# A three-block model in split float32: two of the three products of each up projection and gate joined in one 512-column product

## The chip, the cores and the metric

The kernel runs on one core of a Trainium2 chip. The metric is the device time of one execution in microseconds. The program is one launch that loads all its weights from device memory.

## The reference

Three blocks of width 1024 run over one sequence of 256 tokens, each a mixer followed by a feed-forward. The first mixer holds two attentions over 8 heads, one that keeps 64 keys for each query (picked by an index score) and one over low-rank keys and values; sigmoid gates weigh the two branches:

```python
        y_a = jnp.einsum('bsc,cd->bsd', o_a, w_branch_a[l])
        y_b = jnp.einsum('bsc,cd->bsd', o_b, w_branch_b[l])
        merged = jax.nn.sigmoid(g_a) * y_a + jax.nn.sigmoid(g_b) * y_b
        h = h + jnp.einsum('bsd,de->bse', merged, w_out[l])

        hn = rmsnorm(h, norm_ffn_g[l])
        u = jnp.einsum('bsd,df->bsf', hn, w_up[l])
        u = causal_depthwise_conv(u, conv_w[l], conv_b[l])
        gate, val = jnp.split(u, 2, axis=-1)
        h = h + jnp.einsum('bsf,fd->bsd', jax.nn.silu(gate) * val, w_down[l])
```

The second mixer is a gated linear recurrence, the third an attention with a bias by distance. Their feed-forwards are silu(gate) * val without the convolution. Each feed-forward has 2816 columns of gate and 2816 of val.

## The kernel before, in words

Everything is kept transposed: 128 features on the partitions, 256 tokens along the free axis. A matrix of activations `X` is eight row blocks of [128, 256].

*Split products.* Weights and activations are float32. `Weights` loads a piece of 1024 columns, and cuts it into a high part `H` (a ScalarE copy to float32r) and a low part `L` (a VectorE subtraction); these are the "weight splits" below, 128x1024 rows written to tiles named `r`. Activations are cut in the same way by `hl`. A product then is three TensorE instructions (`mm3`): weight high with activation high, weight high with activation low, weight low with activation high, all summed in PSUM. Each has a weight load of its own.

```python
        m(ps, lhsT=aH, rhs=bH, start=start, stop=False, skip_group_check=True)
        m(ps, lhsT=aH, rhs=bL, start=False, stop=False, skip_group_check=True)
        m(ps, lhsT=aL, rhs=bH, start=False, stop=stop, skip_group_check=True)
```

*Projections.* `proj_t` makes 256 output features: eight row blocks times two column blocks times three products of 256 columns, 48 in all, into one PSUM bank (two halves of 256). There are 8 banks.

*The feed-forward.* `ffn` goes over 11 blocks. `up(j)` projects 256 columns of gate and then 256 of val, scales by 1/rms (`rb2`), applies the convolution in the first block's feed-forward (`conv`), the silu, and multiplies; the result is cut in two parts, `acts[j]`. `down(j)` multiplies 256 rows of the down weights with it into accumulators that stay open over the whole stage: four banks of two halves in the first two feed-forwards, five banks in the last (`final`), which is computed token by token, with 512- and 256-column products. The code says up(j) and then down(j - 1).

*The order of instructions.* The program is recorded first, and `Trace.schedule` puts it in order: a list scheduler that goes by a rough price for each instruction, takes what comes earliest in the recorded order among what is ready on an engine, and gives out buffers (15 `f4`, 23 `r4`, 10 `f2`, 8 `ps`, ...) as they come free. So any change in the recorded work moves other instructions as well. All of them carry one line number in the profile, 428, where they are emitted.

*A store in the first mixer.* `late_setup` makes a table of biases by distance for the third mixer: an 8x384 row in an `f2` buffer, spread by a GpSimd DMA to 1.5 MB in device memory (`dram`). It is recorded after the first mixer, and scheduled among its attentions.

## Time and profile before

| | before |
|---|---|
| time, median of 3 runs | 1055.04 us (1054.74 to 1059.61) |
| span of the profiled execution | 1055.1 us |
| TensorE busy (products) | 1015.7 us, 96% |
| VectorE busy | 720.5 us, 68% |
| ScalarE busy | 533.0 us, 51% |
| TensorE's mean granted clock | 0.987 |

The profiled execution is seen by its span, from its first to its last instruction. A product's own duration is longer than its distance to the next, since products overlap in the engine; a pace has to be read from a count of them in a known time.

The stages in the span: first mixer up to about 227 us, the feed-forward with convolution to about 420, the recurrence to about 576, the second feed-forward to about 757, the third mixer to about 863, the last feed-forward to the end.

### The profile page before, as it was taken

To read this page: it belongs to the slowest core of one execution; us is meant where nothing else is said; L and a number is where in the kernel's file an instruction comes from. 1 tells how busy PE (TensorE), PEld (TensorE's weight loads), DVE (VectorE), ACT (ScalarE), POOL (GpSimd) and SP (SyncE) were. 2 spreads that over 40 slices of the span, in tenths; PEclk is the share of its full clock that TensorE was granted. 3 is DMA by queue.
4 is the path that set the end of the run, shared out by engine and by line. 5 is a ranking of instruction groups with operands and counts; after the bars stand their busy time and mean duration, and the time that the engine had idled before them with its cause. 6 is when DMAs were issued, how large, how long until landed. Compare 5 with 4: busy or idle time off the path is not lost.

```text
span 1055.1 us, 20892 instructions
## 1 busy us (share of the span) xinstructions
PE 1015.7 (96%) x8710; PEld 973.7 (92%) x8710; DVE 720.5 (68%) x1278; ACT 533.0 (51%) x804; POOL 44.7 (4%) x40
## 2 busy tenths in 40 slices
PE   7998499999999999999999999999999999999997
PEld 5876399999999999999999999999989999999996
DVE  7996256768867779887878655555856676556564
ACT  7867244546555557444455444444544655444322
POOL 2000000020000002000002000000200010000000
PEclk9999599999999999999999999999999999999999
DMA  9347355745555565355555565656555555565501
GB/s 325 94 125 164 98 161 160 250 150 163 189 189 183 177 200 160 101 162 167 168 176 153 178 200 162 199 172 197 167 164 174 177 162 178 171 207 171 162 1 40
DMA packets 130688, 174.02 MB, mean 165 GB/s; under 512 B 6163, under 2 KB 113043, under 8 KB 130593
## 3 DMA queue, kind: packets, MB, share of 16 engines
q1 hardware_dynamic: 129312, 169.31, 50.9%
q0 software_dynamic: 1280, 3.37, 1.7%
q8 instruction: 68, 1.11, 0.4%
q14 instruction: 28, 0.22, 0.1%
HBM read 170.04 MB, written 2.62 MB: 164 GB/s over the span
## 4 chain that ended last, share of the span: by engine, by line
PE 88%; DVE 5%; DMA 4%; ACT 1%; POOL 1%; issue 1%; POOLq 0%; DVEq 0%; ACTq 0%
PE ps L428 88%; DMA dram<-f 3%; DVE r L428 3%; DVE f L428 2%; POOL f L428 1%; ACT f L428 1%; DVE fs L428 1%; DVE h L428 1%; DMA f<-in_conv_w_dram 0%; ACT r L428 0%; DVEq L428 0%; POOLq L428 0%; DVE lb L428 0%; ACTq L428 0%; POOLq L1412 0%
## 5 line engine op out<-in xcount | busy, mean ns | idle before, releaser
L428 PE MATMUL ps<-r,r 128*128 128x256 f32 (+3 forms) x7182 | 938.7, 291 | 3.1 <-DVE r L428 2.3
L428 PEld LDWEIGHTS ps<-r,r 128*128 128x128 f32 x7182 | 898.5, 192 | 25.6 <-DVE r L428 4.6
L428 ACT ACTIVATE r<-f 128x1024 fp32r<-128x1024 f32 (+4 forms) x369 | 352.4, 989 | 211.5 <-DVE f L428 100.9
L428 DVE TENSOR_TENSOR r<-f,r 128x1024 fp32r<-128x1024 f32 (+3 forms) x365 | 411.8, 1163 | 53.4 <-PE ps L428 30.9
L428 DVE TENSOR_TENSOR f<-ps,f 128x512 f32<-128x512 f32 (+2 forms) x104 | 70.7, 683 | 171.1 <-PE ps L428 163.9
L428 ACT ACTIVATE f<-f 128x512 f32<-128x512 f32 (+5 forms) x82 | 44.9, 549 | 104.3 <-DVE f L428 98.3
L428 ACT ACTIVATE f<-ps 128x512 f32<-128x512 f32 (+5 forms) x78 | 36.7, 517 | 75.0 <-PE ps L428 74.8
L428 POOL TENSOR_TENSOR f<-f,f 128x512 f32<-128x512 f32 x18 | 30.4, 1691 | 707.3 <-ACT f L428 675.9
L428 DVE TENSOR_TENSOR f<-f,f 128x512 f32<-128x512 f32 (+4 forms) x79 | 49.1, 623 | 10.1 <-PE ps L428 4.6
L428 PE MATMUL ps<-pack,f 128*128 128x128 f32 (+2 forms) x165 | 27.8, 304 | 22.0 <-DVE f L428 18.8
L428 PE MATMUL ps<-f,f 128*64 128x128 f32 (+4 forms) x320 | 48.4, 344 | 0.5 <-ACT f L428 0.5
L428 PEld LDWEIGHTS ps<-pack,f 128*128 128x128 f32 (+2 forms) x165 | 20.8, 152 | 28.1 <-DVE f L428 19.3
L428 PEld LDWEIGHTS ps<-f,f 128*64 128x64 f32 (+3 forms) x320 | 37.0, 176 | 7.8 <-ACT f L428 2.5
L428 ACT ACTIVATE f<-f,vec,cw 128x256 f32<-128x256 f32 x44 | 24.0, 594 | 39.9 <-DVE f L428 39.9
L428 ACT ACTIVATE f<-f,fs 128x256 f32<-128x256 f32 (+3 forms) x50 | 24.4, 489 | 38.6 <-DVE fs L428 38.5
L428 DVE SCALAR_TENSOR_TENSOR f<-f,cw,f 128x255 f32<-128x255 f32 (+1 forms) x88 | 38.2, 478 | 7.1 <-ACT f L428 6.8
L428 DVE CUSTOM_DVE_ANT_0 f<-ps,f 128x256 f32<-128x256 f32 (+1 forms) x48 | 17.6, 398 | 32.8 <-DMA dram<-f 18.4
L428 ACT ACTIVATE f<-ps,fs 128x512 f32<-128x512 f32 (+3 forms) x28 | 15.7, 619 | 24.4 <-PE ps L428 24.3
L428 DVE TENSOR_TENSOR f<-f,fs 128x512 f32<-128x512 f32 (+6 forms) x46 | 16.6, 391 | 8.1 <-PE ps L428 7.5
L428 DVE SCALAR_TENSOR_TENSOR r<-h,vec,r 128x256 fp32r<-128x256 f32 x32 | 21.2, 708 | 0.6 <-ACT r L428 0.6
L428 ACT ACTIVATE r<-h,vec 128x256 fp32r<-128x256 f32 x32 | 14.5, 501 | 12.4 <-DVE h L428 12.4
L428 PEld LDWEIGHTS ps<-f 128*32 128x32 f32 (+2 forms) x880 | 14.0, 114 | 4.2
(84 smaller groups left out, 240.1 us busy)
## 6 DMA issues: line engine op xcount, KB each, us to landing
f<-in_ffn_w_dram SPq DMA_DIRECT2D x132, 512.0 KB, 4.4
f<-in_w_up_dram SPq DMA_DIRECT2D x44, 512.0 KB, 4.6
f<-in_hgrn_w_in_dram SPq DMA_DIRECT2D x32, 512.0 KB, 4.5
f<-in_w_in_dram SPq DMA_DIRECT2D x26, 512.0 KB, 5.4
f<-in_moba_w_in_dram SPq DMA_DIRECT2D x24, 512.0 KB, 4.5
f<-in_w_down_dram SPq DMA_DIRECT2D x22, 512.0 KB, 4.3
f<-in_w_out_dram SPq DMA_DIRECT2D x8, 512.0 KB, 3.5
f<-in_hgrn_w_out_dram SPq DMA_DIRECT2D x8, 512.0 KB, 3.8
```

The lines of the kernel that those rows point to most:

```text
L428: getattr(getattr(self.nc, op.eng), op.fn)(*args, **kwargs)
```

## The change

The two parts of an activation now lie side by side in one tile ([part, row block, token]), so that a row block's high and low part can be the moving operand of one product. The eight gates of the first mixer and all up projections use the new `proj_w` in place of `proj_t`: weight high with both parts is one product of 512 columns into a whole bank (high half, low half), and weight low with activation high is one of 256 columns into the second half. A projection has 32 products, and needs two banks. `sum_w` brings the halves together on the way out: a ScalarE copy of the second half, and a VectorE add of the first. All other projections (`proj_t`, `proj_x`) keep their three products, with new indices. The comments that the full diff also strips are left out here.

```diff
     def parts(self, K):
-        ts = [[self.t("r4", min(4, K - k), SEQ) for k in range(0, K, 4)] for _ in range(2)]
-        return [[t[:, k, :] for t in p for k in range(t.shape[1])] for p in ts], ts
+        ts = [self.t("r4", 2, min(2, K - k), SEQ) for k in range(0, K, 2)]
+        return [t[:, :, k, :] for t in ts for k in range(t.shape[2])], ts
...
-                self.hl(H[hf][:, :, c], L[hf][:, :, c], tmp)
+                for i in range(2):
+                    xt = XT[2 * hf + i]
+                    self.hl(xt[:, 0, :, c], xt[:, 1, :, c], tmp[:, 2 * i:2 * i + 2, :])
...
+    def proj_w(self, W, X, K, n0=0, n=2):
+        pss = [self.ps(2, SEQ) for _ in range(n)]
+        m = self.nc.tensor.matmul
+        for k in range(K):
+            for j, ps in enumerate(pss):
+                H, L = (w[:, n0 + j * P:n0 + (j + 1) * P] for w in W[k])
+                m(ps, lhsT=H, rhs=X[k], start=k == 0, stop=False, skip_group_check=True)
+                m(ps[:, 1], lhsT=L, rhs=X[k][:, 0], start=False, stop=k == K - 1, skip_group_check=True)
+        return pss
+
+    def sum_w(self, pss, dst=None):
+        dst = self.t("f2", 2, SEQ) if dst is None else dst
+        for j, ps in enumerate(pss):
+            part = self.t("f1", SEQ)
+            self.nc.scalar.activation(part, ps[:, 1], AF.Copy)
+            self.nc.vector.tensor_tensor(dst[:, j, :], ps[:, 0], part, op=ALU.add)
+        return dst
...
         def gate(col, dst):
             W = Weights(self, self.rows(w_in, col, col + SEQ))
-            ps = self.ps(2, SEQ)
-            self.proj_t(W, ps, X, 8)
-            V.tensor_tensor(dst, ps, rbc[:, None, :].to_broadcast([P, 2, SEQ]), op=ALU.mult)
+            self.sum_w(self.proj_w(W, X, KD), dst)
+            V.tensor_tensor(dst, dst, rbc[:, None, :].to_broadcast([P, 2, SEQ]), op=ALU.mult)
...
-                ps = self.ps(2, SEQ)
-                self.proj_t(W, ps, X, KD)
-                u = self.t("f2", 2, SEQ)
+                u = self.sum_w(self.proj_w(W, X, KD))
                 if part == 0 or conv:
-                    V.tensor_tensor(u, ps, rb2, op=ALU.mult)
+                    V.tensor_tensor(u, u, rb2, op=ALU.mult)
...
                 else:
-                    V.tensor_tensor(u, ps, us[0], op=ALU.mult)
-                    V.tensor_tensor(u, u, rb2, op=ALU.mult)
+                    V.tensor_tensor(us[0], us[0], rb2, op=ALU.mult)
+                    V.tensor_tensor(u, u, us[0], op=ALU.mult)
```

The order of TensorE in the last feed-forward, where the gate's projection ends and val's begins (a name is PSUM tile <- weights or activations; the shape is the output). Before, gate fills bank `ps_158`, and val begins in `ps_159`:

```order
L428 MATMUL ps_158<-r_85,r_79 128x256
L428 MATMUL ps_158<-r_85,r_83 128x256
L428 MATMUL ps_158<-r_78,r_83 128x256
L428 MATMUL ps_158<-r_85,r_79 128x256
L428 MATMUL ps_159<-r_88,r_82 128x256
L428 MATMUL ps_159<-r_77,r_82 128x256
L428 MATMUL ps_159<-r_88,r_90 128x256
```

Now gate fills `ps_154` and `ps_153`, and val begins in `ps_159`:

```order
L428 MATMUL ps_154<-r_78,r_98 128x256
L428 MATMUL ps_153<-r_78,r_76 128x512
L428 MATMUL ps_153<-r_78,r_98 128x256
L428 MATMUL ps_159<-r_94,r_88 128x512
L428 MATMUL ps_159<-r_94,r_87 128x256
...
L428 MATMUL ps_159<-r_86,r_89 128x256
L428 MATMUL ps_159<-r_86,r_84 128x512
L428 MATMUL ps_154<-r_94,r_88 128x512
L428 MATMUL ps_154<-r_94,r_87 128x256
```

Eleven products of val's first column block go into `ps_159` before the first of its second block goes into `ps_154`, which gate has just used; before, the next bank was another one.

The order of VectorE in the first mixer, around the 8x384 row that the store reads (its buffer is `f_108` before and `f_102` now; 128x1024 rows are weight splits). Before:

```order
L428 TENSOR_SCALAR f_119<-pack_171,fs_139 128x128
L428 TENSOR_TENSOR r_87<-f_64,r_98 128x1024
L428 TENSOR_TENSOR r_78<-f_67,r_83 128x1024
L428 TENSOR_TENSOR f_108<-ps_158,f_70 8x384
L428 TENSOR_TENSOR r_82<-f_60,r_86 128x1024
...
L428 TENSOR_SCALAR f_102<-f_102,fs_138 128x256 x2
L428 ISA f_108,fs_146<-ps_158,f_125 128x256
```

Now:

```order
L428 RECIPROCAL fs_135<-fs_135 128x2
L428 TENSOR_SCALAR lb_205<-lb_201 128x8
L428 TENSOR_TENSOR f_102<-ps_158,f_70 8x384
L428 TENSOR_SCALAR f_106<-f_106,fs_135 128x256 x2
L428 TENSOR_TENSOR r_78<-f_67,r_95 128x1024
...
L428 RECIPROCAL fs_145<-fs_145 128x2
L428 ISA f_102,fs_146<-ps_159,f_117 128x256
```

The row stands behind 12 of the 128x1024 splits before and behind 8 now. In both orders the last row shown, the second pair of heads over the second tile of queries, writes into the buffer that the store reads.

The order of VectorE in the first feed-forward, around val's projection of a block (`f_121` holds 1/rms, `cw` the convolution's weights, and the second operand of the 128x256 rows from `ps` is ScalarE's copy). Before, the scaling reads the bank:

```order
L428 TENSOR_TENSOR f_107<-ps_153,f_126 128x512
L428 TENSOR_TENSOR r_79<-f_64,r_76 128x1024
L428 SCALAR_TENSOR_TENSOR f_104<-f_107,cw_193,f_104 128x255 x2
L428 SCALAR_TENSOR_TENSOR f_104<-f_107,cw_193,f_104 128x254 x2
L428 TENSOR_TENSOR f_104<-f_104,f_109 128x512
```

Now:

```order
L428 TENSOR_TENSOR f_103<-ps_160,f_115 128x256
L428 SCALAR_TENSOR_TENSOR f_105<-f_102,cw_193,f_105 128x254
L428 TENSOR_TENSOR f_103<-ps_159,f_124 128x256
L428 TENSOR_TENSOR f_103<-f_103,f_121 128x512
L428 TENSOR_TENSOR r_82<-f_64,r_83 128x1024
L428 SCALAR_TENSOR_TENSOR f_104<-f_103,cw_193,f_104 128x255 x2
L428 SCALAR_TENSOR_TENSOR f_104<-f_103,cw_193,f_104 128x254 x2
```

Two adds have come in ahead of the scaling, which now reads their sum.

## Rows read from the trace of the kernel before

**Rows 1.** The page: busy microseconds, share of the span and instructions of each engine (PE is TensorE's products, PEld its weight loads, DVE VectorE, ACT ScalarE), and the chain of work that ended last, by engine.

```profile
PE 1015.7 (96%) x8710; PEld 973.7 (92%) x8710; DVE 720.5 (68%) x1278; ACT 533.0 (51%) x804; POOL 44.7 (4%) x40
PE 88%; DVE 5%; DMA 4%; ACT 1%; POOL 1%; issue 1%; POOLq 0%; DVEq 0%; ACTq 0%
```

**Rows 2.** Groups of TensorE's products between 300 and 400 us, by form: line, engine, operation, out<-in, shape, count | busy us, mean ns of one | idle before.

```profile
L428 PE MATMUL ps<-r,r 128*128 128x256 f32 x835 | 100.4, 283 | 0.0
```

**Rows 3.** The same between 765 and 786 us, in the third mixer's values.

```profile
L428 PE MATMUL ps<-r,r 128*128 128x512 f32 x95 | 21.7, 389 | 0.0
```

**Rows 4.** Busy time of each engine in a stretch of each feed-forward (from:to, length, then the engines with their counts, the granted clock, DMA share and GB/s).

```profile
234.00:407.00 173.00, 173.00 (x1443) 172.80 (x1441) 132.80 (x191) 97.55 (x128) 0.00 (x0) 1.00 0.57 181
577.00:745.00 168.00, 168.00 (x1403) 168.00 (x1402) 98.67 (x104) 73.82 (x82) 0.00 (x0) 1.00 0.59 189
863.00:1035.00 172.00, 172.00 (x1303) 165.46 (x1303) 99.77 (x114) 68.02 (x77) 0.00 (x0) 1.00 0.46 144
```

**Rows 5.** Groups of instructions over the whole span, by form.

```profile
L428 DVE TENSOR_TENSOR r<-f,r 128x1024 fp32r<-128x1024 f32 x312 | 378.3, 1240 | 37.6 <-PE ps L428 30.9 <-issue 5.4 <-ACT r L428 1.3
L428 ACT ACTIVATE r<-f 128x1024 fp32r<-128x1024 f32 x312 | 319.4, 1052 | 110.4 <-PE ps L428 87.7 <-issue 13.9 <-ACT r L428 8.6
L428 DVE TENSOR_TENSOR f<-ps,f 128x512 f32<-128x512 f32 x101 | 69.4, 690 | 171.0 <-PE ps L428 163.9 <-ACT f L428 5.2 <-ACT r L428 1.6
L428 DVE TENSOR_TENSOR f<-f,f 128x512 f32<-128x512 f32 x63 | 44.0, 699 | 10.0 <-PE ps L428 4.6 <-ACT f L428 4.0
L428 DVE TENSOR_TENSOR r<-f,r 128x512 fp32r<-128x512 f32 x43 | 29.4, 688 | 15.8 <-ACT r L428 15.8
L428 ACT ACTIVATE f<-ps 128x256 f32<-128x256 f32 x14 | 5.4, 383 | 34.5 <-PE ps L428 34.5
```

**Rows 6.** Instructions in order of time at the end of the program: start us, us, engine, line, operation [idle before].

```profile
1046.33 0.41 DVE L428 TENSOR_TENSOR f<-ps,f 128x256 f32<-128x256 f32 x1
1047.74 0.42 DVE L428 TENSOR_TENSOR f<-ps,f 128x256 f32<-128x256 f32 x1
```

**Rows 7.** Instructions in order of time at the end of the first feed-forward.

```profile
401.28 0.69 DVE L428 TENSOR_TENSOR f<-ps,f 128x512 f32<-128x512 f32 x1 [1.47 <-PE ps L428]
...
406.34 4.09 DVE L428 TENSOR_TENSOR r<-f,r 128x1024 fp32r<-128x1024 f32 x4
406.54 1.58 ACT L428 ACTIVATE r<-f 128x512 fp32r<-128x512 f32 x2 [1.53 <-DVE f L428]
...
407.22 0.73 PE L428 MATMUL ps<-r,r 128*128 128x256 f32 x4 [0.22 <-ACT r L428]
...
408.21 9.98 PE L428 MATMUL ps<-r,r 128*128 128x256 f32 x81 [0.26 <-DVE r L428]
```

**Rows 8.** The first mixer: TensorE's longest wait over the span (engine, tile <- releaser: us in total, times, longest), instructions in order of time on VectorE and GpSimd (POOL), and the store's row among the DMA issues (queue, count, KB, us to landing).

```profile
PE ps L428 <- DVE f L428: 18.8, 3, 17.0
...
31.47 0.42 DVE L428 TENSOR_TENSOR r<-f,r 128x256 fp32r<-128x256 f32 x1
...
82.08 0.54 DVE L428 TENSOR_TENSOR f<-ps,f 8x384 f32<-8x384 f32 x1
...
84.39 3.49 DVE L428 TENSOR_TENSOR r<-f,r 128x1024 fp32r<-128x1024 f32 x3
...
83.32 1.09 POOL L428 DMA_DIRECT2D dram<-f  x1 [64.99 <-ACT r L428]
...
117.94 0.42 DVE L428 CUSTOM_DVE_ANT_0 f<-ps,f 128x256 f32<-128x256 f32 x1 [18.36 <-DMA dram<-f]
...
dram<-f POOLq DMA_DIRECT2D x1, 1536.0 KB, 34.5
```

**Rows 9.** The DMA queues (packets, MB, share of 16 engines; q0 carries the store, q1 the weights) from 84 to 88 us, and q0 from 96 to 100 us.

```profile
q1 hardware_dynamic: 1121, 1.11, 88.1%
q0 software_dynamic: 273, 0.05, 6.7%
...
q0 software_dynamic: 44, 0.20, 49.3%
```

**Rows 10.** Instructions in order of time at the end of the second feed-forward.

```profile
740.23 0.69 DVE L428 TENSOR_TENSOR f<-ps,f 128x512 f32<-128x512 f32 x1 [0.71 <-PE ps L428]
...
742.77 1.58 ACT L428 ACTIVATE r<-f 128x512 fp32r<-128x512 f32 x2 [3.22 <-DVE f L428]
743.43 2.99 DVE L428 TENSOR_TENSOR r<-f,r 128x512 fp32r<-128x512 f32 x3 [0.78 <-ACT r L428]
```

More of the change, by code (lines that the diff above doesn't have):

```diff
@@ L541, in parts @@
     def parts(self, K):
-        ts = [[self.t("r4", min(4, K - k), SEQ) for k in range(0, K, 4)] for _ in range(2)]
-        return [[t[:, k, :] for t in p for k in range(t.shape[1])] for p in ts], ts
+        ts = [self.t("r4", 2, min(2, K - k), SEQ) for k in range(0, K, 2)]
+        return [t[:, :, k, :] for t in ts for k in range(t.shape[2])], ts
     def pair(self):
-        t = self.t("r4", 2, 2, SEQ)
-        return [[t[:, p, k, :] for k in range(2)] for p in range(2)], t
+        X, ts = self.parts(2)
+        return X, ts[0]
     def bcast(self, col):
@@ L599, in begin @@
         nc = self.nc
-        X, (H, L) = self.parts(KD)
+        X, XT = self.parts(KD)
         turned = []
@@ L892, in mixer1 @@
         krT = self.t("fs", 2, 32)
-        (cq, cqt), (ckv, (ckh, ckl)) = self.pair(), self.parts(1)
+        (cq, cqt), (ckv, ckt) = self.pair(), self.parts(1)
         psk = self.ps(SEQ)
@@ L982, in mixer1 @@
             c = slice(t * P, (t + 1) * P)
-            self.hl(obt[0][0][:, :, c], obt[1][0][:, :, c], ob)
+            for i in range(2):
+                self.hl(obt[i][:, 0, :, c], obt[i][:, 1, :, c], ob[:, 2 * i:2 * i + 2, :])
         pss = chunk(512, 768)
```

15 lines of the change are left out of this document (8 added, 7 removed).

## The prediction

> **What bounds the kernel now.** I read the busy times first, then the chain of waits, then TensorE's stretches one by one. The busy times [rows 1] put TensorE at 96% of the span, VectorE at 68%, ScalarE at 51%, and the chain that ended last is TensorE for 88%. A busy TensorE is not yet a TensorE at its peak, so the second reading is the pace: in a stretch with nothing but 128x256 products, 835 of them make 100.4 us busy, and a single one lasts 283 ns [rows 2]. From first start to last start that is (100.4 - 0.283) / 834 = 0.1200 us each. In a stretch of 128x512 products, 95 make 21.7 us at 389 ns each [rows 3]: (21.7 - 0.389) / 94 = 0.2267 us each. The second has 256 columns more and costs 0.1067 us more, so columns run at 0.417 ns (the 2.4 GHz level; the granted clock is 1.00 there) and 0.0133 us of every product, with its weight load, belongs to the instruction and not to its columns. TensorE issues without a gap in the three feed-forward stages: in a long window of each it is busy 173 of 173, 168 of 168 and 172 of 172 us [rows 4]. So a product less is time less, as long as no other engine falls behind. The two places where TensorE does wait are the first mixer (17.0 us once, released by VectorE, rows 8) and the seams between stages.
>
> **The change, part by part.**
>
> *Fewer, wider products.* Each projection of 256 columns has 8 x 2 groups (eight row blocks, two column blocks). A group had three products of 256 columns, 3 x 0.1200 = 0.3600 us; now it has one of 512 and one of 256, 0.2267 + 0.1200 = 0.3467 us. The columns are the same 768; one instruction and one weight load go. That is 0.0133 us a group. There are 3 x 11 x 2 = 66 projections in the feed-forward stages and 8 gates, 74 x 16 = 1184 groups: 1184 x 0.0133 = **15.8 us** (14.1 in the feed-forward stages, 1.7 in the gates). Bounds: no row shows a 512-column product between 256-column ones, nor one whose moving operand is two pieces. If its fixed cost doubled with its width it would take 2 x 0.1200 = 0.2400 us, and nothing would be saved. If the product behind it had its weights loaded wholly under the long one and cost only its columns, 0.1067 us, the saving would double to 31.5 us. I take 0.2267, the measured pace of the same width and type.
>
> The Trainium skill speaks against this size: "TensorE: Matmul & The Clock Gate", section "Wait — 56ns, not 53.3ns?", gives a warm matmul a fixed cost of about 2.5 ns. By that figure 1184 products fewer would be worth an estimated 3 us, and the change would hardly show. The trace disagrees [rows 2, 3]: here the cost beyond the columns is 13.3 ns at both widths, with a weight load in front of every product.
>
> *The sums on the way out.* Each projection now adds two ScalarE copies of 128x256 out of PSUM (383 ns [rows 5]) and two VectorE adds of 128x256 with a PSUM operand (0.41 to 0.42 us [rows 6]); the scaling of 128x512 stays, from SBUF instead of PSUM, 699 instead of 690 ns [rows 5]. What hides them is idle time of both engines under TensorE. The tightest stage is the first feed-forward, with the convolution: its block is 144 products, 17.29 us, so the window of 173 us is 10.0 blocks [rows 4], VectorE busy 132.80 / 10.0 = 13.3 us a block and ScalarE 9.8. The block shrinks by 32 x 0.0133 to 16.86 us; VectorE gets 4 x 0.415 more, 14.9 us (89%), ScalarE 4 x 0.383, 11.3 us (67%). In the second feed-forward VectorE has 98.67 us in 9.7 blocks, 10.1 us, and comes to 11.8 (70%). So no engine passes TensorE, and I cost the sums at nothing there; without this cover they would be 148 x (0.383 + 0.415) = 118 us of work.
>
> *The seams.* At a stage's end the last block's sums lie on the path. In the first feed-forward the last scaling starts at 401.28 and TensorE has only the next-to-last down projection as cover (48 x 0.1200 = 5.8 us); it waited 0.22 + 0.26 us for the activations' parts [rows 7]. The chain now gets a copy and an add in front, 0.383 + 0.415 = 0.8 us, plus a handover: 0.9 us, exposed in full since the cover was already used up. A copy that comes just behind a weight split of 1.05 us on ScalarE would make it 2.0; below nothing is excluded, as something is only added. In the other two feed-forwards the cover still has room: in the second the low parts are written by 743.43 + 0.69 = 744.1 us and the products that need them start one down projection after the last up product, 740.2 + 5.8 = 746.0 [rows 10], so 1.9 us against 0.9 more. I take nothing there (bound 1.1 us if a copy sits behind a split). **+0.9 us.**
>
> *Two banks a projection.* The first and second feed-forward keep four accumulators, so four banks are left, two projections, and between a bank's two uses lie a whole down projection and the other projection; an eviction of 1 to 3 us is covered. The last one keeps five accumulators: three banks are left, and the second projection of a block finds one free. The order shows what the scheduler does with it: 11 products into the free bank before the first into the bank just used. They are 6 x 0.2267 + 5 x 0.1200 = 1.96 us, and the used bank had its last product 0.35 us before the projection's end: 2.3 us of cover. The eviction is a copy and an add, 0.8 us with idle engines; behind a split just begun on each (1.052 and 1.240 us [rows 5]) it is 3.1 us. So 0 to 0.8 us a block, 0 to 9 us in 11 blocks. That stage's block is 17.0 us, so the window of 172 us is 10.1 blocks [rows 4]; with the sums VectorE comes to 99.77 / 10.1 + 1.7 = 11.5 us of 16.6 (69%) and ScalarE to 8.3 (50%), so most evictions start at once: I take **0**.
>
> *The first mixer.* The changed order also moves the 8x384 row that feeds the distance table's store. Before, VectorE writes it at 82.08, GpSimd issues the store at 83.32, and it lands 34.5 us later; VectorE waits 18.36 us for it at 117.94, since its next exponent wants the same buffer, and TensorE waits with it [rows 8]. In the changed order the same pair of heads takes the store's buffer, so the wait remains. But four weight splits fewer stand ahead of the row (1.16 us each, three in 3.49 [rows 8]), and eight half-size splits of activations (0.42 us) in place of four of 0.69 [rows 5, 8]: 4 x 1.16 - (8 x 0.42 - 4 x 0.69) = 4.0 us earlier, if VectorE is what sets the pace there. How much of it comes out? From 84 to 88 us the store moved 0.05 MB while the weights' queue held the engines at 88%, and 0.20 MB in each later 4 us [rows 9]. It really starts when the weights stop, about 88 us, and the weights are as many as before. So four more microseconds of that trickle bring it 0.05 MB forward, 1 us. Bounds: 0 and 4.5 us earlier, or 1 us later by the extra halves at the beginning. **-1.0 us.**
>
> **Sum.** Against the profiled execution's span, 1055.1 us (the runs shown have their median at 1055.04, so no correction): 1055.1 - 15.8 + 0.9 + 0 - 1.0 = 1039.2. Rounded up for small handovers at the five other seams, **1039.5 us**.
>
> **Rivals.**
> *Three banks stall.* In the last feed-forward most evictions come behind splits: up to 0.8 us x 11 = 9 us, 1048. For it: VectorE and ScalarE serve both in order, and weight splits are their commonest row [rows 5]. Against: VectorE is idle a third of that stage, and ScalarE half.
> *The products do not get cheaper.* The 512-column product costs 0.2400 us or the next one waits for its weights 13 ns longer: nothing is gained, 1055.1 + 0.9 - 1.0 = 1055. For it: weight loads are busy 92% [rows 1], so the load may be the pace at 256 columns, and a 256-column product still follows each wide one. Against: 512-column products pay the same 13.3 ns though their loads have twice the time. The fixed cost of 2.5 ns in the Trainium skill's page would land in the same case, near 1052.
> *VectorE becomes the bound in the first feed-forward* (the other side). Its adds stand in order behind a copy on ScalarE, which may itself wait out a split of 1.052 us. If each of the four adds of a block waits 1.052 + 0.383 = 1.43 us at the head of VectorE's queue, a block takes 13.3 + 4 x (1.43 + 0.415) = 20.7 us instead of 17.29, 11 x 3.4 = +37 us; the other stages still save 15.8 x 52 / 74 = 11.1: 1055.1 + 37 - 11 = 1081. It decides from 18.3 us a block on, where the loss equals the saving elsewhere: (18.3 - 13.3) / 4 - 0.415 = 0.84 us of waiting for each add. Against: the order puts weight splits between a projection's end and its adds, so the wait is filled, and VectorE already waits in this order for TensorE.
> *The better case.* The second product's load is hidden and part of its 13.3 ns goes too, or the store lands 4 us earlier: 1030 to 1036.
>
> **How the numbers follow.** The forecast (1036 to 1045) 0.64; the better case 0.10; three banks stall, or half of VectorE's waits (1045 to 1050) 0.11; nothing cheaper (1050 to 1060) 0.08; VectorE the bound (over 1060) 0.07. The range from 1032 to 1050 leaves out about 0.18: the last two cases and the far end of the better one. The likeliest case's own range is 1036 to 1045. Half a percent, about what a measurement here can tell from no change, is 5.3 us. Faster by more than that (under 1049.8): 0.84. Within it: 0.08; slower: 0.08.
>
> **What the profile of the changed kernel would show.** In a stretch of the first or second feed-forward TensorE has no gap, and a block's 112 products (32 wide, 80 narrow) take 16.9 us; an interval of 17.3 says that the products did not get cheaper. VectorE's share there rises from 77% to about 89%. New TensorE waits on VectorE for a PSUM bank, repeated every 16 to 17 us in the last feed-forward, would be the three-bank rival; TensorE waits on VectorE's low weight parts in the first feed-forward would be the other. The wait at the first mixer's store should end near 117 us. The forecast is wrong if the pace of the pair is not 0.347 us, or if TensorE's waits in the feed-forward stages add up to more than a few microseconds.

## The result, and the profile after

| | median | runs | lowest to highest |
|---|---|---|---|
| kernel before, beside it | 1056.1 us | 9 | 1054.74 to 1060.33 |
| changed kernel | 1062.49 us | 9 | 1060.25 to 1066.38 |

The ratio is 1.0052, 95% interval 1.0035 to 1.0069: the change makes the kernel slower by half a percent. The forecast was 1039.5 (1032 to 1050), faster. The profiled executions have spans of 1055.1 before and 1059.8 after; the readings below explain these 4.7 us.

The page after, busy times, to be read beside [rows 1]:

```profile
PE 1009.9 (95%) x7526; PEld 913.6 (86%) x7526; DVE 773.7 (73%) x1434; ACT 579.1 (55%) x960; POOL 43.1 (4%) x40
```

TensorE has 1184 products fewer, but is busy only 5.8 us less (1015.7 to 1009.9), where the forecast had 15.8. Its idle time, span less busy, went from 39.4 to 49.9 us, 10.5 more. So there are two questions: where 10 us of the gain stayed, and where 10.5 us of idle time came from.

*The pace.* TensorE's products by form in the dense part of the second feed-forward, 588 to 760 us:

```profile
L428 PE MATMUL ps<-r,r 128*128 128x256 f32 x863 | 151.2, 283 | 0.0
L428 PE MATMUL ps<-r,r 128*128 128x512 f32 x295 | 104.7, 399 | 0.0
```

The same stretch by engines (from:to, length, busy times with counts, granted clock, DMA share, GB/s):

```profile
588.00:760.00 172.00, 172.00 (x1158) 158.33 (x1157) 119.55 (x153) 90.28 (x132) 3.45 (x2) 1.00 0.58 185
```

There is no gap (172 of 172 us), as foreseen. Of the 1158 products 295 are wide; 295 narrow ones belong to them, and the other 568 run at the 0.1200 us of [rows 2]. The pair takes (172 - 568 x 0.1200) / 295 = 0.352 us, not 0.3467; a window's edges and missing records leave some 0.002 open. A wide product lasts 399 ns here and 389 in [rows 3].

*The waits.* TensorE's longest wait after (releaser: in total, times, longest):

```profile
PE ps L428 <- ACT f L428: 22.3, 2, 22.2
```

The 17.0 us of VectorE in [rows 8] are gone; 22.2 us of ScalarE stand in their place. Engines in order of time in the first mixer:

```profile
114.93 1.06 ACT L428 ACTIVATE r<-f 128x1024 fp32r<-128x1024 f32 x1 [23.56 <-DMA f<-in_w_in_dram]
115.90 1.06 ACT L428 ACTIVATE f<-ps 128x512 f32<-128x512 f32 x2
116.53 2.07 PE L428 MATMUL ps<-f,f 64*128 64x256 f32 x4 [22.17 <-ACT f L428]
...
231.55 0.39 PE L428 MATMUL ps<-ones,f 128*32 128x1 f32 x16 [2.41 <-POOL f L428]
```

ScalarE stands 23.56 us before a weight split whose weights have not landed, and the evictions that TensorE needs stand behind it in its queue. The row with `ones` (a product that sums over features for the norm) marks the end of the first mixer: 231.55 us. The same two places in the kernel before:

```profile
119.40 1.12 PE L428 MATMUL ps<-pack,f 128*128 128x128 f32 x4 [16.99 <-DVE f L428]
...
227.40 0.31 PE L428 MATMUL ps<-ones,f 128*32 128x1 f32 x16 [2.36 <-POOL f L428]
```

The end of the mixer comes 4.15 us later, of 4.7 in all. The wait itself ends sooner than before (116.53 for 119.40), but it begins sooner still: the last product ahead of it ends at 94.4 us instead of 102.4, with that much less of the mixer done. While TensorE stands, its granted clock falls: from 100 to 112 us it is 0.50, the 1.2 GHz level (before from 108 us on).

*The end of the first feed-forward,* VectorE and TensorE, beside [rows 7]:

```profile
404.80 0.75 DVE L428 TENSOR_TENSOR f<-ps,f 128x256 f32<-128x256 f32 x2
405.47 1.22 DVE L428 TENSOR_TENSOR r<-f,r 128x1024 fp32r<-128x1024 f32 x1
406.60 0.69 DVE L428 TENSOR_TENSOR f<-f,f 128x512 f32<-128x512 f32 x1
407.20 1.22 DVE L428 TENSOR_TENSOR r<-f,r 128x1024 fp32r<-128x1024 f32 x1
408.42 1.76 DVE L428 SCALAR_TENSOR_TENSOR f<-f,cw,f 128x255 f32<-128x255 f32 x4
410.10 1.22 DVE L428 TENSOR_TENSOR r<-f,r 128x1024 fp32r<-128x1024 f32 x1
411.23 0.69 DVE L428 TENSOR_TENSOR f<-f,f 128x512 f32<-128x512 f32 x1
...
412.69 1.60 PE L428 MATMUL ps<-r,r 128*128 128x256 f32 x5 [2.83 <-ACT r L428]
```

Three weight splits of 1.22 us stand between the links of the last block's chain (sum, scaling, convolution, product); TensorE waits 2.83 us where it waited 0.22 + 0.26. Behind the second feed-forward it waits 1.65 us, where it waited 0.46 (after, then before):

```profile
762.56 2.66 PE L428 MATMUL ps<-r,r 128*128 128x256 f32 x15 [1.65 <-DVE r L428]
...
757.78 1.94 PE L428 MATMUL ps<-r,r 128*128 128x256 f32 x14 [0.46 <-DVE r L428]
```

At the end of the third mixer it waits 1.04 us (none before), released by GpSimd; no sum was added there.

The account of idle time: first mixer +6.2, first feed-forward +2.4, second +1.2, third mixer +1.0, second mixer -0.3; together +10.5. Of busy time: the pairs at 0.3533 give 1184 x 0.0067 = -7.9; the other +2.1 is what the next reading bears on.

*The clock behind the waits.* Three microseconds right behind the wait of 2.83 us, and the same place in the kernel before (columns as in [rows 4]; the granted clock is the third number from the end):

```profile
412.70:415.70 3.00, 3.00 (x13) 2.92 (x14) 0.95 (x2) 0.00 (x0) 0.00 (x0) 0.50 0.80 229
...
408.21:411.21 3.00, 3.00 (x25) 3.00 (x26) 2.88 (x4) 0.14 (x1) 0.00 (x0) 1.00 0.74 235
```

The granted clock is 0.50 there, and 13 products of 256 columns pass where 25 do at 1.00. The same happens in three more places, behind waits of 2.25, 2.41 and 1.65 us: from 64.4 to 67.7, 231.7 to 235.0 and 764.1 to 767.5 us the clock is 0.50, and in none of the four was it so in the kernel before. At half the pace each place costs an estimated 1.7 us, 6.8 in all, more than the +2.1. Before, a wait of 2.36 us (at 227.40) was not followed by a fall, so what decides it is not shown. Over all runs the mean granted clock is 0.978 to 0.983 in the changed kernel and 0.983 to 0.990 in the kernel before beside the experiments.

My theory after this reading: (1) something in the pair costs 0.0067 us; (2) the new layout changes the first mixer's order, and the slow store there makes a loss of it; (3) the extra hops (handovers from one engine to the next) let weight splits into the chains at the ends. The rivals: the gates' pairs cause the first mixer's loss, or the change loses by itself whatever the store does.

In the runs below the ratios are to runs of the kernel before on the same chip, whose medians lay between 1055.0 and 1058.3 us.

### The profile page after: what moved, and what is told of

It reads as the page before. It is cut to its first block, busy times and chain, and to the rows that moved or that the text cites. A ratio compares the mean times of both kernels' runs of the same rounds, so it can differ in the third digit from the quotient of the medians.

```text
span 1059.8 us, 18724 instructions
## 1 busy us (share of the span) xinstructions
PE 1009.9 (95%) x7526; PEld 913.6 (86%) x7526; DVE 773.7 (73%) x1434; ACT 579.1 (55%) x960; POOL 43.1 (4%) x40
## 4 chain that ended last, share of the span: by engine, by line
PE 85%; DVE 8%; DMA 4%; issue 1%; ACT 1%; POOL 1%; ACTq 0%; DVEq 0%; POOLq 0%
PE ps L428 85%; DVE r L428 4%; DMA f<-in_w_in_dram 3%; DVE f L428 3%; DVE h L428 1%; DVE fs L428 1%; POOL f L428 1%; DMA f<-in_conv_w_dram 1%; ACT f L428 0%; ACT r L428 0%; ACTq L428 0%; DVEq L428 0%; DVE lb L428 0%; POOLq L428 0%; POOLq L1434 0%
## 5 line engine op out<-in xcount | busy, mean ns | idle before, releaser
L428 PE MATMUL ps<-r,r 128*128 128x256 f32 (+2 forms) x5998 | 932.7, 316 | 6.6 <-ACT r L428 3.5
L428 PEld LDWEIGHTS ps<-r,r 128*128 128x128 f32 x5998 | 837.4, 191 | 81.6 <-DVE r L428 4.9
L428 ACT ACTIVATE r<-f 128x1024 fp32r<-128x1024 f32 (+2 forms) x373 | 353.4, 980 | 139.1 <-PE ps L428 63.2
L428 ACT ACTIVATE f<-ps 128x256 f32<-128x256 f32 (+5 forms) x226 | 92.1, 426 | 206.2 <-PE ps L428 205.5
L428 DVE TENSOR_TENSOR f<-ps,f 128x256 f32<-128x256 f32 (+2 forms) x178 | 79.9, 464 | 114.9 <-ACT f L428 103.8
L428 DVE TENSOR_TENSOR f<-f,f 128x512 f32<-128x512 f32 (+3 forms) x153 | 99.5, 653 | 13.1 <-ACT f L428 6.3
L428 PE MATMUL ps<-f,f 128*64 128x128 f32 (+4 forms) x320 | 49.9, 349 | 22.3 <-ACT f L428 22.3
L428 ACT ACTIVATE r<-h,vec 128x256 fp32r<-128x256 f32 x32 | 14.4, 501 | 11.5 <-DVE h L428 11.4
L428 PE MATMUL ps<-f 128*32 128x16 f32 (+3 forms) x880 | 17.7, 191 | 0.0
```

The source lines that it names most:

```text
L428: getattr(getattr(self.nc, op.eng), op.fn)(*args, **kwargs)
```

## Experiments: what a pair costs

**Products alone.** Blocks of 64 groups each over the same operands. The forms, for `X` in two pieces and `C` in one:

```
m(ps, lhsT=H, rhs=X[k]);  m(ps[:, 1], lhsT=L, rhs=X[k][:, 0])        # in turn
m(ps, lhsT=H, rhs=C[k]);  m(ps[:, 1], lhsT=L, rhs=C[k][:, 0])        # operand in one piece
m(ps, lhsT=H, rhs=X[k]);  m(ps[:, 0], lhsT=L, rhs=X[k][:, 0])        # first half
```

> Products alone: the kernel does only the first steps of the setup (x, its two parts, and the two parts of 512 columns of w_up), copies the two parts of X also into tiles in which the parts of one k lie side by side, and then runs blocks of 64 groups each on TensorE, every operand on the chip; all else of the computation is left out. In order: twice the three narrow products of the kernel before; the change's pair, its wide operand in two pieces of 256 that are 512 words apart; the pair with the operand in one piece; the pair in two pieces with the narrow product added to the first half; the two wide products of two columns first and then their two narrow ones, in two pieces and then in one piece; wide products alone in two pieces, and in one; narrow products alone; three narrow again. The three narrow should take 23.0 us a block (64 x 0.360) and narrow alone 7.7 by every theory. Two pieces cost (my first theory): the pair takes 22.6 (0.3533) in two pieces and 22.2 (0.3467) in one, whatever its order and half, and wide alone 14.9 against 14.5. Adding to the half just written costs: the pair is 22.6 in two pieces and in one, 22.2 in the first half and with the crossed orders, and wide alone 14.5 in both. The change of width costs: pairs are 22.6 whichever way with wide and narrow in turn, wide alone 14.5 in both, and crossed orders lie between.

VectorE's copies mark the end of every 16 groups, so the distance of two starts is 16 groups. Two marks each, in order, of: three narrow; in turn; one piece; first half; crossed (W W N N); wide alone; narrow alone.

```profile
54.40 0.78 DVE L428 COPY f<-ps 128x256 f32<-128x256 f32 x2 [4.97 <-PE ps L428]
60.16 0.79 DVE L428 COPY f<-ps 128x256 f32<-128x256 f32 x2 [4.97 <-PE ps L428]
...
77.23 0.79 DVE L428 COPY f<-ps 128x256 f32<-128x256 f32 x2 [4.88 <-PE ps L428]
82.89 0.78 DVE L428 COPY f<-ps 128x256 f32<-128x256 f32 x2 [4.88 <-PE ps L428]
...
99.85 0.77 DVE L428 COPY f<-ps 128x256 f32<-128x256 f32 x2 [4.88 <-PE ps L428]
105.50 0.77 DVE L428 COPY f<-ps 128x256 f32<-128x256 f32 x2 [4.88 <-PE ps L428]
...
122.46 0.77 DVE L428 COPY f<-ps 128x256 f32<-128x256 f32 x2 [4.88 <-PE ps L428]
128.11 0.79 DVE L428 COPY f<-ps 128x256 f32<-128x256 f32 x2 [4.88 <-PE ps L428]
...
145.15 0.76 DVE L428 COPY f<-ps 128x256 f32<-128x256 f32 x2 [4.82 <-PE ps L428]
150.72 0.76 DVE L428 COPY f<-ps 128x256 f32<-128x256 f32 x2 [4.82 <-PE ps L428]
...
185.76 0.75 DVE L428 COPY f<-ps 128x256 f32<-128x256 f32 x2 [2.87 <-PE ps L428]
189.39 0.76 DVE L428 COPY f<-ps 128x256 f32<-128x256 f32 x2 [2.87 <-PE ps L428]
...
209.54 0.76 DVE L428 COPY f<-ps 128x256 f32<-128x256 f32 x2 [1.26 <-PE ps L428]
211.46 0.76 DVE L428 COPY f<-ps 128x256 f32<-128x256 f32 x2 [1.16 <-PE ps L428]
```

5.76, 5.66, 5.65, 5.65, 5.57, 3.63 and 1.92 us for 16 groups: 0.3600, 0.3533, 0.3533, 0.3533, 0.3484, 0.2267 and 0.1200. Each product alone costs what [rows 2, 3] gave, and the pair costs 0.0067 more than their sum. Neither the two pieces nor the half matters; my first theory, that the two pieces cost, fell. Had each change of width the same price, crossed order, with half as many changes, should have come to 0.350.

**One piece, in place.**

```diff
-        ts = [self.t("r4", 2, min(2, K - k), SEQ) for k in range(0, K, 2)]
-        return [t[:, :, k, :] for t in ts for k in range(t.shape[2])], ts
+        ts = [self.t("r4", min(2, K - k), 2, SEQ) for k in range(0, K, 2)]
+        return [t[:, k] for t in ts for k in range(t.shape[1])], ts
...
```

> The changed kernel with the two parts of each k side by side in the tiles of X, so that the wide product reads one run of 512 words; every engine has the same order of instructions. If the two pieces cost, the pair falls from 0.3533 to 0.3467 us and 1184 of them give 7.9 us: 1054.6. If the half or the change of width costs, it stays at 1062.5. Splits written in two runs of 256 words could cost VectorE and ScalarE up to 0.05 us each, which is hidden by every theory but at the ends of the feed-forwards.

1062.03 us, ratio to before 1.0046 (1.0029 to 1.0064): nothing gained, as in the run alone.

**Other orders,** over four columns:

```
"turn": "W0N0W1N1W2N2W3N3", "two": "W0W1N0N1W2W3N2N3",
"four": "W0W1W2W3N0N1N2N3", "late": "W0W1N0W2N1W3N2N3"
```

> Products alone, as in the first such run (all else of the computation is left out), 128 groups a block, operands as in the change: wide and narrow in turn; in turn, with the narrow product into another bank; two wide, two narrow; four wide, four narrow; each narrow product one place behind the next wide one (W0 W1 N0 W2 N1 W3 N2 N3); in turn again. The sum of the two alone is 0.3467 a group, 44.4 us a block; in turn took 0.3533, 45.2 us. If the change of width costs, another bank changes nothing (45.2), two and two is 44.6 as before, four and four 44.4 to 44.5, and one place behind, which changes width as often but for the ends, 45.0. If it is that the narrow product adds to what the wide one just before it wrote, another bank gives 44.4 to 44.6, and so does one place behind.

For 32 groups: in turn 11.31 us (0.3533), narrow into another bank 11.14 to 11.28, two and two 11.15 (0.3484), four and four 11.22, one place behind 11.31, and then in turn again, now 11.09: 0.3467. The first and last blocks have the same order of widths and differ by just the cost looked for. None of the theories says so. What differed were the banks, and what ran ahead.

**Banks held fixed:** the same products over eight tiles that are kept throughout.

```
for sets in (("0123", "4567"), ("0246", "1357"), ..., ("01", "23"), ("02", "13"), ...):
    sweep("turn", sets)
```

> Products alone once more (all else of the computation is left out): wide and narrow in turn, 128 groups a block, each block over other PSUM banks, which are named 0 to 7 in the order of their tiles: over banks 0 1 2 3 and then 4 6 7 5 in turn, then 0 2 4 7 and 1 3 6 5, then the first order again, then 0 4 1 6 and 2 7 3 5, then two banks at a time: 0 1 and 2 3, 0 2 and 1 3, 0 4 and 1 6, once more 0 2 4 7 and then 0 1; at the end two wide and two narrow over 0 1 and over 0 2. In the run on orders the first block (banks side by side) took 0.3533 a group and the last (every second bank), with the same order of widths, 0.3467. If neighbouring banks cost, blocks over 0 1 take 45.2 us each time and those over 0 2 take 44.4. If the cost depends on how the products fell into step at the start of a block, the same banks give now 45.2 and now 44.4, or all blocks 45.2.

Every 32 groups in turn took 11.31 us, over neighbouring banks or not (34 intervals, the start left out), and the eight of two and two 11.15. The banks are out.

**What ran ahead.**

```
for form in ("three", "turn", "late", "turn", "turn", "three", "turn", "two", "turn", "late", "turn"):
    sweep(form, ("0123", "4567"))
```

> Products alone (all else of the computation is left out), 128 groups a block over the same banks throughout: three narrow, in turn, one place behind, in turn, in turn, three narrow, in turn, two and two, in turn, one place behind, in turn. In the run on orders a block in turn behind three-narrow work took 0.3533 a group and one behind the block 'one place behind' took 0.3467. If what ran just before sets how products fall into step, and they keep it, blocks in turn take 45.2, then 44.4 and 44.4 (behind one place behind), 45.2 (behind three narrow), 44.4 again at the end; behind two and two it may be either. If the faster block had another cause, all blocks in turn take 45.2.

Fixed banks, and a mark every 32 groups, two each from: in turn behind three narrow; in turn behind one place behind; in turn behind three narrow again; in turn behind two and two.

```profile
101.94 0.42 DVE L428 COPY f<-ps 128x256 f32<-128x256 f32 x1 [10.88 <-PE ps L428]
113.25 0.42 DVE L428 COPY f<-ps 128x256 f32<-128x256 f32 x1 [10.89 <-PE ps L428]
...
180.66 0.42 DVE L428 COPY f<-ps 128x256 f32<-128x256 f32 x1 [10.67 <-PE ps L428]
191.76 0.42 DVE L428 COPY f<-ps 128x256 f32<-128x256 f32 x1 [10.67 <-PE ps L428]
...
327.22 0.42 DVE L428 COPY f<-ps 128x256 f32<-128x256 f32 x1 [10.89 <-PE ps L428]
338.53 0.42 DVE L428 COPY f<-ps 128x256 f32<-128x256 f32 x1 [10.89 <-PE ps L428]
...
405.30 0.42 DVE L428 COPY f<-ps 128x256 f32<-128x256 f32 x1 [10.67 <-PE ps L428]
416.39 0.42 DVE L428 COPY f<-ps 128x256 f32<-128x256 f32 x1 [10.67 <-PE ps L428]
```

11.31, 11.10, 11.31 and 11.09. So one and the same sequence in turn runs at either of two paces and keeps the one it starts with (for 256 groups behind one place behind): 0.3533 behind narrow products, 0.3467 behind a block of another order. That the history sets the pace is shown; what state in TensorE holds it is not. The Trainium skill, "TensorE: Matmul & The Clock Gate", section "Step-by-step: what each phase is for", says that the engine may take a weight load ahead of products still running. How far ahead the loads run would be such a state; no run here shows it.

**Crossed order, in place.**

```diff
         for k in range(K):
-            for j, ps in enumerate(pss):
-                H, L = (w[:, n0 + j * P:n0 + (j + 1) * P] for w in W[k])
+            HL = [[w[:, n0 + j * P:n0 + (j + 1) * P] for w in W[k]] for j in range(n)]
+            for ps, (H, L) in zip(pss, HL):
                 m(ps, lhsT=H, rhs=X[k], start=k == 0, stop=False, skip_group_check=True)
+            for ps, (H, L) in zip(pss, HL):
                 m(ps[:, 1], lhsT=L, rhs=X[k][:, 0], start=False, stop=k == K - 1, skip_group_check=True)
```

> The changed kernel with two wide products (of two output columns, into two banks) ahead of their two narrow ones. Alone on TensorE that order took 0.3484 us a group for 0.3533. If that holds in place, 1184 groups give 5.8 us: 1056.7 against 1062.5, the three dense feed-forwards alone 5.2 us. If what surrounds the products eats it (sums that end later on ScalarE and VectorE, another order in the first mixer), it stays within 1060 to 1063.

1056.67 us, where 1056.7 was expected; to before 1.0000 (0.9987 to 1.0013). Products by form in the dense part of the second feed-forward, 588 to 758 us:

```profile
L428 PE MATMUL ps<-r,r 128*128 128x256 f32 x856 | 125.5, 281 | 0.0
L428 PE MATMUL ps<-r,r 128*128 128x512 f32 x296 | 93.0, 395 | 0.0
```

By the same count as before the pair takes (170 - 560 x 0.1200) / 296 = 0.347 us, where it took 0.352 in turn, and a wide product lasts 395 ns instead of 399.

## Experiments: the first mixer and its store

**The gates back to three narrow products.**

```diff
-            self.sum_w(self.proj_w(W, X, KD), dst)
-            V.tensor_tensor(dst, dst, rbc[:, None, :].to_broadcast([P, 2, SEQ]), op=ALU.mult)
+            ps = self.ps(2, SEQ)
+            self.proj_t(W, ps, X, KD)
+            V.tensor_tensor(dst, ps, rbc[:, None, :].to_broadcast([P, 2, SEQ]), op=ALU.mult)
```

> The changed kernel with the gates of the first mixer in three narrow products into one bank, scaled from PSUM by one instruction, as before the change; the layout of X and the feed-forwards stay changed. If the pairs and sums of the gates caused the first mixer's loss, the ones row at the end of that mixer comes at 227.4 to 228.5 instead of 231.55 and the kernel takes some 1059.5. If the new layout of X, which the start of this mixer writes in four splits for two, moved the store of the position biases and what waits for it, the row stays at 231 to 233 and the time at 1062 to 1063.

1061.92 us (1.0056, 1.0036 to 1.0075); the `ones` row at 232.75, TensorE's wait 21.9 us. The gates are not the cause.

**The change in the feed-forwards alone:** in the first mixer, narrow gates as in the last run, and the parts in tiles of their own.

```diff
-        X, XT = self.parts(KD)
+        X, (H, L) = self.parts_apart(KD)
...
-                for i in range(2):
-                    xt = XT[2 * hf + i]
-                    self.hl(xt[:, 0, :, c], xt[:, 1, :, c], tmp[:, 2 * i:2 * i + 2, :])
+                self.hl(H[hf][:, :, c], L[hf][:, :, c], tmp)
...
```

> The change in the three feed-forwards alone: the first mixer has the tiles, the splits and the narrow gates of the kernel before, and TensorE's and ScalarE's orders there are those of before, row for row. If the new layout in the first mixer made its loss, the ones row at its end comes at 227.4 for 231.55, and the kernel takes 1062.5 - 4.15 = 1058.3, within 0.2% of before. If the feed-forwards themselves lost, it stays over 1061; if they gain the forecast 14.1, it takes 1043.

The `ones` row in order of time:

```profile
227.02 0.30 PE L428 MATMUL ps<-ones,f 128*32 128x1 f32 x16 [2.41 <-POOL f L428]
```

TensorE's waits by releaser:

```profile
PE ps L428 <- DVE f L428: 20.0, 4, 17.4
...
PE ps L428 <- ACT r L428: 2.8, 1, 2.8
```

1054.54 us, 0.9985 (0.9967 to 1.0003). The first mixer ends where it did before, with the wait of 17 us on VectorE again; the 2.8 us at the end of the first feed-forward stay. With the run before it this decides against the gates: the layout, with the order of instructions that comes with it, made the first mixer's loss. In the four profiled kernels with the new layout and the slow store in the first mixer that mixer ends at 230.2 to 233.0 us, in the two with the old layout at 227.0 and 227.4.

**The store later:** its loads, its product and itself behind the first feed-forward, in the changed kernel and in the one before.

```diff
+    def late_rel(self):
+        end = len(nc.ops) - 1
...
+        nc.gpsimd.dma_start(rel, a["c_rel"]).deps[end] = True
...
+        b.late_rel()
         X = b.mixer2(X)
```

> The changed kernel with the loads for the position biases, their product and the 1.5 MB store moved behind the first feed-forward; nothing reads them before the third mixer. If the store of 34 us keeps the weights away from the first mixer, TensorE's wait of 22.2 us there falls to under 8, the first mixer ends 10 to 20 us sooner and the kernel takes 1043 to 1055, with what the store then takes from the second mixer's weights to be seen in its waits (0 to 8 us). If the wait comes from the order of ScalarE's work alone, the first mixer's end moves by under 3 us.

> The kernel before, with the loads, the product and the store of the position biases moved behind the first feed-forward, as in the run of the changed kernel that took 1052.7. Both kernels then have a first mixer without that store. If the change loses only where the store and its order of ScalarE's work meet in the first mixer (+4.15 us there, +0.55 in all else by the two traces), this kernel takes 1052 to 1055. If the new layout costs the first mixer time without the store too, or the pairs' gain is eaten elsewhere, it takes 1049 or less.

1052.7 us changed (0.9960, 0.9938 to 0.9982), 1059.75 before (1.0025, 1.0009 to 1.0042). The first mixer ends at 208.28 and 212.08, 23 and 15 us sooner. Both pay it back in the second mixer, unequally: the changed kernel's longest wait there is 7.4 us, the other's is this one, again on ScalarE behind weights:

```profile
459.95 1.06 ACT L428 ACTIVATE r<-f 128x1024 fp32r<-128x1024 f32 x1 [19.92 <-DMA f<-in_hgrn_w_in_dram]
462.88 2.93 PE L428 MATMUL ps<-f,f 128*128 128x256 f32 x8 [17.17 <-ACT f L428]
```

With the store there the change gains 7.0 us, with it in the first mixer it loses half a percent. So its sign hangs on which order meets the store.

**The store in two steps,** in both kernels: the table goes to device memory once (`short`), and is spread from there. The longer arguments are cut to `...`.

```diff
-        nc.gpsimd.dma_start(self.scr.rearrange(...), rb[:, None, :].to_broadcast([8, P, REL_W]))
+        short = nc.tile("short", [1, 8 * REL_W]).rearrange("o (h x) -> (o h) x", x=REL_W)
+        nc.gpsimd.dma_start(short, rb)
+        nc.gpsimd.dma_start(self.scr.rearrange(...), short[:, None, :].to_broadcast([8, P, REL_W]))
```

> The changed kernel with the store of the position biases in two steps: 12 KB from 8 partitions to DRAM, then 1.5 MB from there to its place in DRAM, 128 times the same row for each head. If reading from 8 partitions makes the store slow (34 us for 1.5 MB), it takes under 15 us, TensorE's wait of 22.2 us falls under 8 and the time to 1045 to 1053. If writing 1024 rows is what takes the time, it stays at some 34 us and the time at 1060 to 1064.

> The kernel before with the store of the position biases in two steps, 12 KB to DRAM and from there 128 times over; the changed kernel with the same edit took 1038.2. If the change itself is worth what the pair's 0.3533 us gives less the ends of the feed-forwards (7.9 less some 5), or the 7.0 that lay between the two kernels with the late store, this kernel takes 1041 to 1046. If the change loses time without the slow store too, it takes 1038 or less.

In the changed kernel, the two DMAs (queue, count, KB, us to landing):

```profile
dram<-short POOLq DMA_DIRECT2D x1, 1536.0 KB, 14.4
...
short<-f POOLq DMA_DIRECT2D x1, 12.0 KB, 3.3
```

And the `ones` row:

```profile
207.82 0.31 PE L428 MATMUL ps<-ones,f 128*32 128x1 f32 x16 [1.03 <-POOL f L428]
```

1038.17 us changed (0.9821, 0.9789 to 0.9852), 1038.29 before (0.9816, 0.9792 to 0.9841). The first mixer ends at 207.82 and 205.32, 24 and 22 us sooner. The weights' queue in the changed kernel from 84 to 100 us (packets, MB, share of 16 engines), with the store from 8 partitions and with the store in two steps:

```profile
q1 hardware_dynamic: 809, 0.80, 16.1%
...
q1 hardware_dynamic: 2724, 2.71, 57.8%
```

The loads of 512 KB issued in that time take 29.9 us to land beside the slow store, and 8.1 beside the quick one. My number for the kernel before (1041 to 1046) was wrong: with the quick store four runs each (1033.8 to 1039.5 changed, 1035.7 to 1038.8 before) show no difference, though by the two intervals a gain or loss of some 4 us could hide. The clock may eat part of the cheaper pairs here too: its mean is 0.990 to 0.994 in the runs of the changed kernel and 0.995 to 0.997 in those of the other, which is an estimated 5 us of 1038.

The Trainium skill, "DMA: Bandwidth & Descriptors", section "Issuing engines are not separate DMA queues", says that queues of all engines share the same 16 DMA engines; the 0.80 MB agree. That reading from the 8 partitions is the slow side follows from the times: the store took 33.7 to 34.9 us from there, and 12.1 to 14.4 us with the same writes from device memory.

## Experiments: both together, and the ends

**Crossed order and two-step store.**

> The changed kernel with the two-step store and two wide products ahead of their two narrow ones. If both edits add up (-24 and -5.8 of 1062.5), 1032 to 1033. If the crossed order's gain in the run before came from the order in the first mixer, it is nearer to 1038.

1030.68 us (0.9759, 0.9736 to 0.9782): 7.5 less than in turn with the same store, and 7.6 less than the kernel before with it. So with crossed order the change does pay, beside the kernel before with the same store.

**Only the first k crossed.**

```diff
+            for f, j in ((wide, 0), (wide, 1), (narrow, 0), (narrow, 1)) if k == 0 else ((wide, 0), (narrow, 0), (wide, 1), (narrow, 1)):
+                f(j)
```

> The changed kernel with the two-step store; of the eight k of each two columns only the first has two wide products ahead of their two narrow ones, all others are in turn as in the change. Alone, products in turn kept 0.3467 a group behind a block of two and two and 0.3533 behind narrow ones. If they keep it in place too, a dense stretch of the feed-forwards takes 0.3467 a group, and the kernel 0.0067 x 1184 = 7.9 us less than in turn throughout (1038.2): 1030, like crossed order throughout (1030.7) or up to 2 us less. If the step is lost between products of the real kernel, it stays at 0.353 a group and 1036 to 1039.

1035.65 us (0.9787, 0.9762 to 0.9811). The dense parts of the first two feed-forwards give 0.348 and 0.3485 a pair by the same count (0.352 in turn throughout, 0.347 crossed), and 396 ns a wide product: between both paces. The trace shows that one crossed k helps; by the medians it is 2.5 us, which lies within the spread of the four and five runs. Why the pace does not come down as far as behind a whole block alone was not tried.

**The last block narrow,** on top of crossed order and two-step store.

```diff
+                if j < NB - 1:
+                    u = src = self.sum_w(self.proj_w(W, X, KD))
+                else:
+                    u, src = self.t("f2", 2, SEQ), self.ps(2, SEQ)
+                    self.proj_t(W, src, X, KD)
...
```

> As the run with two-step store and crossed order, but the last block of each feed-forward in three narrow products into one bank, as before the change. If the two more hops between ScalarE and VectorE at the end of the last block, each of which lets a weight split of 1.22 us in ahead of the chain, make the ends wait (2.83 for 0.48 us behind the first feed-forward, 1.65 for 0.46 behind the second), these waits fall back and, less 96 pairs at 0.0116 us lost, the kernel is 1.5 to 2.5 us faster than the run without this edit. If the splits stand in the chain for another reason, the waits stay and it is 1 us slower.

TensorE at the end of the first feed-forward in the run with crossed order and two-step store:

```profile
385.32 16.50 PE L428 MATMUL ps<-r,r 128*128 128x256 f32 x110 [3.92 <-ACT r L428]
```

And in the run with the last block narrow:

```profile
389.50 0.74 PE L428 MATMUL ps<-r,r 128*128 128x256 f32 x4 [0.22 <-ACT r L428]
390.50 1.70 PE L428 MATMUL ps<-r,r 128*128 128x256 f32 x12 [0.25 <-DVE r L428]
```

The waits fall back to those of [rows 7]: the extra hops let the splits in. From one `ones` row to the next the first feed-forward takes 193.2 us instead of 196.1, the second 184.4 instead of 185.3. The time does not show it: 1031.45 us (0.9755, 0.9728 to 0.9783), a miss. The mean granted clock differs from run to run by more than this edit is worth: 1027.5 us came at 0.997, 1036.4 at 0.990.

**The same two with the first mixer as before:** the edit of the run on the feed-forwards alone on top.

> The change in the feed-forwards alone, with the crossed order there, and the two-step store. The first mixer is that of the kernel before with this store, whose ones row came at 205.3; with the whole change and crossed order it came at 205.7, in turn at 207.8. If the new layout costs the first mixer time only through the slow store, this takes 1030 to 1032, like the whole change with these two edits (1030.7). If the layout costs it 2 to 4 us of its own, 1027 to 1029.

> As the run beside it, with the last block of each feed-forward in three narrow products. If the ends of the feed-forwards are what is left of the loss, it is 1 to 2.5 us faster than that run (waits of 3.9 and 0.5 us less, 96 pairs at 0.0116 us more). If what is saved there comes back as waits or a lower clock behind it, it takes the same within 1 us.

1031.72 us (0.9761, 0.9732 to 0.9789) and 1030.56 (0.9751, 0.9721 to 0.9781). The medians show no cost of the layout without the slow store. The traces leave some room: the first mixer ends at 206.4 and 205.7 here and at 205.3 in the kernel before, with the new layout at 205.7, 207.8, 210.0 and 211.7. The ends are worth 1.8 and 0.8 us by the `ones` rows and 1.2 by the medians, which six runs that spread over 5 to 10 us cannot decide; between 1030.6 and 1031.7 these four kernels are the same.

## Why the prediction was wrong

*Fewer, wider products* failed in its largest term: 0.3467 us a pair was the sum of two paces measured apart, and in place it is 0.3533. 7.9 us came of the 15.8. The bounds named (0 and 31.5) held the value, but the choice between them took for granted that two paces add up. The rival "products do not get cheaper" named the half-truth, though not for its reason: the load alone does not set the pace, since the same weights and operands run at 0.3467 behind another order.

*The sums* were right: VectorE is at 146.59 of 172 us (85%) in the first feed-forward, where 89% was forecast, and TensorE has no gap there. *Three banks* cost nothing: no wait recurs in the last feed-forward. *VectorE the bound* did not come.

*The seams* failed by size. The step took one copy, one add and a handover as the whole addition, +0.9 at one seam and nothing at the others; it came to +2.4 and +1.2 behind the first two feed-forwards, and to nothing behind the last. What it left out is that every further hop between ScalarE and VectorE opens a place where a split of 1.22 us goes ahead. Another +1.0 came behind the third mixer, where no hop was added; why is not shown.

*The first mixer* failed in sign: -1.0 was forecast, +4.15 came. The row did come 4 us earlier, as worked out (store issued at 79.70 for 83.32), and landed earlier. TensorE's wait also ended where the forecast had it, near 117 us (116.53), though released by ScalarE and not by VectorE, so the number was met for another reason. But the step said that the wait for the store's buffer remains and asked only when it ends, not when it begins: it began 8 us sooner, with that much less done. In the new order ScalarE meets a weight split first whose weights are queued beside the store, and waits longer than VectorE had. The step looked at the engine that waited before, not at who else hangs on the queue that the store fills.

*The clock* had no term. The sum left it as it was before; in four places it was now at 0.50 behind short waits, an estimated 6.8 us.

By the terms: 1039.5, +7.0 for the 1056 pairs of the feed-forwards, +6.9 for the first mixer (-1.0 and -1.7 for its gates became +4.15), +3.4 for the seams (0.9 and the rounding of 0.3 became 4.6, the 1.0 behind the third mixer with them): 1056.8. The span is 1059.8, 3.0 us more. Three of the four places at the low clock lie behind the first mixer's end, an estimated 5.1 us; they cover the 3.0, and the 2 us that then came back are not placed on rows.

## What to carry to other kernels

Two paces measured apart need not add up: when instructions of different length are to alternate, look for a stretch that alternates, or time the sequence by itself, and try its order, since crossing two pairs gave 5.8 us here for nothing. A change that pays a few microseconds can be outweighed by whichever in-order engine now meets a slow transfer first, so take the slow transfer out of the way before judging the change. Where a chain at a stage's end gets another hop, count one interposed instruction of the neighbours for it, not the hop alone, and look at the granted clock behind the wait that results: here the slow restart cost an estimated 1.7 us behind waits of 1.65 to 2.83.

## What was not expected of the hardware

- A sequence of 512- and 256-column products in turn has two steady paces, 0.3533 and 0.3467 us a pair with every operand the same, and keeps the one that it falls into.
- Weight load and product together cost 13.3 ns beyond their columns at both widths, alone as in [rows 2, 3] (0.1200 and 0.2267 us). The Trainium skill's fixed cost of 2.5 ns, "TensorE: Matmul & The Clock Gate", section "Wait — 56ns, not 53.3ns?", does not appear in these sequences.
- A DMA of 1.5 MB from 8 partitions took 33.7 to 34.9 us and let the other queue move 0.80 MB in 16 us; from device memory it took 12.1 to 14.4 and left it 2.71 MB.
- Waits of 1.65 to 2.83 us were followed by a granted clock of 0.50 in four places of the changed kernel (13 products in 3 us for 25), but a wait of 2.36 us in the kernel before was not.
